# A decoder layer on one core: entry norms in tile order, q strips traced before the next tiles' transposes, v copied by ScalarE, row sums of squares on GpSimd

## The chip, the core and the metric

One core of a Trainium2 chip runs the whole layer. The time is device microseconds of one launch: 1199.61 us is the median of three runs of the kernel before (1198.49 to 1199.99). The core has a matrix engine (TensorE; PE in the profile, PEld for its weight loads), a vector engine (VectorE, DVE), a scalar engine (ScalarE, ACT), GpSimd (POOL), and the queue of SyncE (SP), which issues most of the DMAs. ScalarE issues DMAs too (ACTq in the profile).

## The reference, cut to what matters

All arrays are float32; 1024 tokens, width 1024, 16 heads of 64, of which 8 do stick-breaking attention (sb) and 8 sliding-window attention (swa, with two key/value heads).

```python
h = layer_norm(x, ln_in_g, ln_in_b)
proj = h @ w_in                     # [sb_q | sb_k | sb_v | swa_q | swa_k | swa_v]
sb_out, swa_out = stick_breaking_attention(...), sliding_window_attention(...)
mix = concat([rms_norm(sb_out, g_sb), rms_norm(swa_out, g_swa)]) @ w_out
h = layer_norm(ALPHA * h + mix, ln1_g, ln1_b)
ffn = (silu(h @ w_gate) * (h @ w_up)) @ w_down
out = layer_norm(ALPHA * h + ffn, ln2_g, ln2_b)
```

`rms_norm` divides each token's row of 512 by the root of the mean of its squares; the kernel keeps `sb_out` and `swa_out` transposed (features on partitions), so the sum of squares of a token runs over partitions and strips.

## The kernel before, in words

Each matrix operand is split into a high part (fp32r) and a low part, and a product is three matmuls (`mm3`, L169). Weights come as strips of 128 columns (`strip`, L201, two ahead): SP loads a raw strip into one of two staging buffers, ScalarE casts the high part (L108), GpSimd subtracts the low part (L109).

Entry. SP loads the norm's gain and bias as rows and the first x tiles; TensorE broadcasts the rows over the partitions (L269) and ScalarE copies the four halves out (L270). `entry(t)` (L303) norms the token tile t: VectorE takes the statistics (L141 to L134), GpSimd the power -1/2 (L135). For tiles 0 and 1 VectorE does all the scaling (L151, L154); for the others ScalarE subtracts the mean (L161), VectorE scales (L162) and GpSimd adds the bias (L164). Then TensorE transposes the tile in two groups of four (L117), ScalarE casts the high part (L121), TensorE subtracts it in PSUM (L124) and ScalarE casts the low part (L125). Last, ScalarE's queue stores h (L314). The transposes use two PSUM buffers.

First projections (L554 to L568). For each of four chunks of 256 tokens (two tiles): the swa k strip (`put_k`), the v strip (`put_v`, L339: VectorE copies the product out of PSUM, L343, TensorE transposes it, L346), then `entry` of the next two tiles, the two q strips of the first key/value head, and, from the second chunk on, two blocks of the first attention. Later stages interleave attention (`swa_attend`, `sb_attend`) with the next projections by `merge`, which weighs steps of both. The v of the four pairs of sb heads comes in two chunks of 512 each.

Output projections. `c1_steps` (L598) projects the swa half while the last sb pair's attention runs; then follows the sb half (L646 to L673) with the second norm and the transposes for the feed-forward part. `out_load(g, c)` (L505) loads four strips of one chunk of 256 tokens, casts the high part (ScalarE, L510), subtracts the low part (VectorE, L511) and squares in place (ScalarE, L512). `out_proj` (L515) sums a tile's squares by TensorE against a column of ones, one matmul per strip (L522, in the profile two records each), takes the root (L525, L528), and then does the tile's products (L174), which VectorE scales and adds (L533). Two chunks are loaded ahead.

A planner puts each engine's instructions in order: it runs over a simulated timeline and takes, of those that are ready, the one traced first (attention steps inside `merge` get a head start). The order is then fixed per engine; at run time an engine waits for the next one in its order. `Ordered` (L50) can tie the instructions of one queue to the order in which they are traced; before, it is on for SP in the last stage alone (L813).

Of the kernel before, what the change touches and what calls it, by code (L numbers as in the profile page):

```python
# [49 lines left out]
class Ordered:  # L50
# [12 lines left out]

    def matmul(self, *a, **k):
        self._queue(self.eng.matmul(*a, **k))

    def transpose(self, *a, **k):
        self._queue(self.eng.transpose(*a, **k))

    def dma_start(self, *a, **k):  # L70
        self._queue(self.eng.dma_start(*a, **k))


@with_exitstack
def layer(ctx: ExitStack, tc: tile.TileContext, x, ln_in, w_sw, w_sb, norm_g,
          sinks, rel_bias, onehot, w_out, ln1, w_gu, w_down, ln2, out):
    nc = tc.nc
    pe, act, dve, pool = nc.tensor, nc.scalar, nc.vector, nc.gpsimd
    sp = Ordered(tc, nc.sync)
# [27 lines left out]
    def split_w(raw, hi, lo):  # L107
        act.copy(hi, raw)  # L108
        pool.tensor_tensor(out=lo, in0=raw, in1=_f(hi), op=ALU.subtract)  # L109

    def split_ps(ps, hi, lo):
# [25 lines left out]
    def ln_stats(xt, n=2, eps=LN_EPS):  # L137
        bst = st.tile([P, n, 6], F32, tag=f"bst{n}", name="bst")
        w = D // n
        for i in range(n):  # L140
            dve.bn_stats(out=bst[:, i, :], in_=xt[:, i * w:(i + 1) * w])  # L141
        mv = st.tile([P, 2], F32, tag="mv", name="mv")
        dve.bn_aggr(out=mv, in_=bst)  # L143
        rstd = st.tile([P, 1], F32, tag="rstd", name="rstd")
        rpow(rstd, mv[:, 1:2], 1.0, eps)
        return mv[:, 0:1], rstd

    def ln_apply(dst, xt, g, b, fast=False, eps=LN_EPS):
        mu, rstd = ln_stats(xt, 2, eps)
        if fast:  # L150
            dve.scalar_tensor_tensor(out=dst, in0=xt, scalar=mu, in1=g, op0=ALU.subtract, op1=ALU.mult)  # L151
            for i in range(2):
                h = slice(i * 512, i * 512 + 512)
                dve.scalar_tensor_tensor(out=dst[:, h], in0=dst[:, h], scalar=rstd, in1=b[:, h],  # L154
                                         op0=ALU.mult, op1=ALU.add)
            return
        nmu = st.tile([P, 1], F32, tag="nmu", name="nmu")
        dve.tensor_scalar(out=nmu, in0=mu, scalar1=-1.0, scalar2=None, op0=ALU.mult)
        for i in range(2):
            h = slice(i * 512, i * 512 + 512)  # L160
            act.activation(dst[:, h], xt[:, h], AF.Identity, bias=nmu)  # L161
            dve.scalar_tensor_tensor(out=dst[:, h], in0=dst[:, h], scalar=rstd, in1=g[:, h],  # L162
                                     op0=ALU.mult, op1=ALU.mult)
            pool.tensor_tensor(out=dst[:, h], in0=dst[:, h], in1=b[:, h], op=ALU.add)  # L164

    def bc_load(dst, src):
# [34 lines left out]
    def strip(i, ahead=2):  # L201
        while len(loaded) < min(len(strips), i + ahead):
            i_ = len(loaded)
            raw = w_raw(strips[i_])
            hi, lo = (U([P, KT, P], "whu"), U([P, KT, P], "wlu")) if i_ == 3 else w_tiles()
            split_w(raw, hi, lo)
            loaded.append((hi, lo))
        return loaded[i]
# [57 lines left out]
    for i, dst in enumerate((g_in, b_in)):  # L266
        for h in (slice(0, 512), slice(512, D)):
            ps = bps.tile([P, 512], F32, tag=("pp", "av")[i], name="bc")
            pe.matmul(ps, row1, rows[i][:, h], start=True, stop=True)  # L269
            act.copy(dst[:, h], ps)  # L270
    sink = cst.tile([P, 8], F32, name="sink")
# [30 lines left out]

    def entry(t):  # L303
        xt = xts.pop(t)
        ln_apply(xt, xt, g_in, b_in, t < 2)
        c, o, todo = t // 2, (t % 2) * P, []
# [6 lines left out]
        flush(todo)  # L313
        act.dma_start(h_dram[t], xt)  # L314

# [23 lines left out]
    def put_v(ps, c0, nc_, vts):  # L339

        n = 2 * nc_
        vr = ws.tile([P, n, P], F32, tag="raw", bufs=2, name="vr")
        dve.tensor_copy(vr.rearrange("p a b -> p (a b)"), ps)  # L343
        pv = bps.tile([P, n, 2, 64], F32, tag="pp", name="pv")
# [160 lines left out]
    def out_load(g, c):  # L505
# [6 lines left out]
        act.activation(m, m, AF.Square)  # L512
        return mh, ml, m

    def out_proj(c, m, wo, acc):  # L515
        mh, ml, ss = m
        for i in range(2):
            t = 2 * c + i
            tok = slice(i * P, (i + 1) * P)
            pr = bps.tile([P, 1], F32, tag="pp", name="pr")  # L520
            for k in range(4):
                pe.matmul(pr, ss[:, k, tok], ones, start=(k == 0), stop=(k == 3))  # L522
            var = st.tile([P, 1], F32, tag="var", name="var")
# [29 lines left out]
    att0 = swa_attend(0, q0, kd, kl, vts, bias0)  # L553
    entry(0)  # L554
    entry(1)
    for c in range(4):
# [3 lines left out]
        put_v(ps, c, 1, vts)  # L560
        if c < 3:
            entry(2 * c + 2)
            entry(2 * c + 3)
        swa_q(0, 0, q0, c, 1)
        swa_q(0, 1, q0, c, 1)
        if c > 0:
            next(att0)
# [23 lines left out]
    def load_acc(c, src):  # L591
# [4 lines left out]
        return res  # L596

    def c1_steps():  # L598
        ms = [out_load(1, 0), out_load(1, 1)]
        for c in range(4):  # L600
# [3 lines left out]
            if c < 2:  # L604
                ms.append(out_load(1, c + 2))

    merge(sb_attend(NPAIR - 1, *cur), 72, c1_steps(), 8)
# [38 lines left out]
    order = (0, 2, 1, 3)  # L646
    ms = {c: out_load(0, c) for c in order[:2]}
    hs = {}
# [220 lines left out]
    with tc.tile_pool(name="dn", bufs=4, reuse_waits="tile") as dn:  # L869
# [8 lines left out]
        def one(t):  # L878
            ot = dn.tile([P, D], F32, tag="ot", bufs=2, name="ot")
            rows = slice(t * P, (t + 1) * P)  # L880
            if t < NT - 1:
                ln_apply(ot, h[t], g2, b2)
                nc.sync.dma_start(out[rows, :], ot)
                return
            mu, rstd = ln_stats(h[t], 4)
            for x in (d0, d1):
# [103 lines left out]
```

## Time and profile before

| | us |
|---|---|
| median of three runs | 1199.61 |
| the profiled execution | 1199.59 |
| its span, first to last instruction | 1197.9 |
| TensorE busy | 1154.2 |
| VectorE busy | 837.7 |
| GpSimd busy | 591.8 |
| ScalarE busy | 581.3 |
| mean granted TensorE clock | 0.986 |

The span is cut into stages by what TensorE works on: the entry and first projections until about 100 us, attention with projections until about 380, the output projections until about 560, then the feed-forward part. A busy TensorE is not a TensorE at its peak: matmuls are pipelined, their ends are modelled, and at the lower clock level they take longer.

### The profile page before, as it was taken

The page shows a single profiled execution, that of the slowest core. Times are in us where ns is not written, and L with a number is a line of the kernel's source. Part 1 is how long each engine was busy: PE and PEld are TensorE (multiplying, and loading weights), DVE is VectorE, ACT ScalarE, POOL GpSimd, SP SyncE. Part 2 cuts the span into 40 slices and gives each one's busy share as a digit, 9 for nine tenths or more (in the row PEclk, how much of TensorE's full clock was granted, in tenths as well). Part 3 has the DMA queues.
Part 4 walks back from the last instruction along what each step waited for, and adds up shares of the span by engine and source line. Part 5 has one row for each costly group of instructions (what it writes and reads, how often), then busy time and mean ns, then how long its engine had stood idle before and what let it go on. Part 6 is the DMA issues. An engine that isn't in the chain of part 4 may idle for free. (4 is left out here: it accounts for less than half of the span.)

```text
span 1197.9 us, 17900 instructions
## 1 busy us (share of the span) xinstructions
PE 1154.2 (96%) x6394; PEld 997.9 (83%) x6394; DVE 837.7 (70%) x1291; ACT 581.3 (49%) x1255; POOL 591.8 (49%) x572
## 2 busy tenths in 40 slices
PE   6899999999998998998999999999999999999997
PEld 4888998999998887876888888888888888888885
DVE  8776687887889895866765555564565448899735
ACT  5666577767677654346333232223233224456531
POOL 5623435566646463214777657665577521000584
PEclk9999999999999998999999999999999999999999
DMA  7403012110105525243333223422232339853431
GB/s 249 167 15 93 27 28 76 28 62 25 48 19 182 196 93 191 83 141 141 114 132 114 89 79 115 131 90 96 97 114 97 106 111 388 328 185 106 131 123 70
DMA packets 59913, 140.17 MB, mean 117 GB/s; under 512 B 7046, under 2 KB 18863, under 8 KB 59825
## 3 DMA queue, kind: packets, MB, share of 16 engines
q1 hardware_dynamic: 45264, 110.19, 28.6%
q10 hardware_dynamic: 14560, 28.85, 6.2%
q8 instruction: 50, 0.82, 0.3%
q14 instruction: 39, 0.31, 0.1%
HBM read 95.23 MB, written 41.17 MB: 114 GB/s over the span
## 5 line engine op out<-in xcount | busy, mean ns | idle before, releaser
L109 POOL TENSOR_TENSOR w<-s,w 128x512 fp32r<-128x512 f32 x88 | 124.0, 1412 | 121.4 <-ACT w L108 121.4
L174 PE MATMUL pp<-xh,whi 128*128 128x256 f32 x544 | 157.3, 290 | 1.4 <-DVE q L337 1.4
L174 PE MATMUL pp<-xh,wlo 128*128 128x256 f32 x544 | 157.0, 289 | 0.0
L174 PE MATMUL pp<-xl,whi 128*128 128x256 f32 x544 | 156.6, 288 | 0.0
L108 ACT CAST w<-s 128x512 fp32r<-128x512 f32 x88 | 54.6, 622 | 201.9 <-PE pgu L730 119.9
L803 PE MATMUL pd<-bhl,ahl 128*128 128x512 f32 x612 | 139.2, 389 | 0.0
L803 PEld LDWEIGHTS pd<-bhl,ahl 128*128 128x128 f32 x612 | 114.8, 188 | 24.2 <-DVE bhl L795 0.4
L762 DVE TENSOR_TENSOR t<-t,pgu 128x512 f32<-128x512 f32 x88 | 60.0, 682 | 98.7 <-PE pgu L730 95.6
L454 POOL TENSOR_TENSOR s<-s,s 128x127 f32<-128x127 f32 (+2 forms) x96 | 91.5, 956 | 51.8 <-DVE s L450 25.0
L174 PEld LDWEIGHTS pp<-xh,whi 128*128 128x128 f32 x544 | 105.5, 194 | 2.5 <-DVE q L337 1.7
L174 PEld LDWEIGHTS pp<-xl,whi 128*128 128x128 f32 x544 | 105.2, 193 | 1.5 <-ACT xl L125 0.3
L174 PEld LDWEIGHTS pp<-xh,wlo 128*128 128x128 f32 x544 | 105.2, 193 | 1.3
L795 POOL TENSOR_TENSOR ahl<-ar,ahl 128x512 fp32r<-128x512 f32 x12 | 16.2, 1353 | 134.8 <-ACT ahl L794 134.7
L450 DVE TENSOR_TENSOR_SCAN s<-s,brk 128x128 f32<-128x128 f32 (+1 forms) x64 | 69.4, 1089 | 12.0 <-ACT s L441 11.2
L794 ACT CAST ahl<-ar 128x512 fp32r<-128x512 f32 x63 | 39.1, 622 | 77.1 <-PE pd L803 50.2
L112 ACT CAST at<-tra 128x256 fp32r<-128x256 f32 (+1 forms) x160 | 55.2, 355 | 36.4 <-DVE at L113 19.0
L395 POOL TENSOR_TENSOR L<-L,rd 128x512 f32<-128x512 f32 (+1 forms) x32 | 30.9, 988 | 81.7 <-DVE rd L393 80.0
L109 POOL TENSOR_TENSOR w<-gr,w 128x512 fp32r<-128x512 f32 x44 | 62.2, 1424 | 8.1 <-ACT w L108 8.1
L113 DVE TENSOR_TENSOR at<-tra,at 128x256 fp32r<-128x256 f32 (+1 forms) x160 | 58.8, 382 | 8.8 <-ACT at L112 7.5
L730 PE MATMUL pgu<-B11h,w 128*128 128x512 f32 x176 | 59.1, 397 | 2.1 <-ACT w L108 1.5
L441 ACT ACTIVATE s<-z 128x128 f32<-128x128 f32 (+2 forms) x96 | 47.6, 498 | 23.9 <-PE z L440 15.7
L730 PE MATMUL pgu<-T4h,w 128*128 128x512 f32 x176 | 57.9, 390 | 0.4 <-DVE t L762 0.4
(234 smaller groups left out, 3315.6 us busy)
## 6 DMA issues: line engine op xcount, KB each, us to landing
ar<-a_dram SPq DMA_DIRECT2D x73, 256.0 KB, 3.1
a_dram<-act ACTq DMA_DIRECT2D x33, 512.0 KB, 2.6
gr<-in_w_gu SPq DMA_DIRECT2D x24, 512.0 KB, 3.4
ur<-in_w_gu SPq DMA_DIRECT2D x23, 512.0 KB, 3.5
bq<-in_w_down SPq DMA_DIRECT2D x44, 256.0 KB, 5.2
raw<-in_w_sb SPq DMA_DIRECT2D x12, 512.0 KB, 3.6
h_dram<-x ACTq DMA_DIRECT2D x8, 512.0 KB, 5.2
m<-o_dram SPq DMA_DIRECT2D x32, 128.0 KB, 2.8
```

The lines of the kernel that those rows point to most:

```text
L108: act.copy(hi, raw)
L109: pool.tensor_tensor(out=lo, in0=raw, in1=_f(hi), op=ALU.subtract)
L112: act.copy(hi, ps)
L113: dve.tensor_tensor(out=lo, in0=ps, in1=_f(hi), op=ALU.subtract)
L174: pe.matmul(ps, a, b, start=(i == 0), stop=(i == n - 1))
L441: act.activation(s2[:, 0:w], ps, AF.Sigmoid, scale=-SCALE)
L450: dve.tensor_tensor_scan(s2[:, 0:w][:, ::-1], s2[:, 0:w][:, ::-1], brk[:, 512 - w:][:, ::-1] if last else zero.broadcast_to([P, w]), 1.0 i ...
L454: pool.tensor_tensor(out=s1[:, 0:m], in0=s1[:, 0:m], in1=s2[:, 1:m + 1], op=ALU.mult)
L730: pe.matmul(ps, a, b, start=(start and n == 0), stop=(stop and n == 11), skip_group_check=True)
L762: add = lambda out, x: dve.tensor_tensor(out=out, in0=x, in1=ps, op=ALU.add)
L794: act.copy(w[:, 0], src)
L803: pe.matmul(pd[t], x, y, start=(first and k == 0 and n == 0), stop=(end and k == KF - 1 and n == 2), skip_group_check=True)
```

## The change

The entry is cut into `norm(t)` and `turn_in(t)` (the transposes). `norm(t)`'s statistics are tied behind the last VectorE instruction that tile t-1's norm returns (for tiles 0 and 1 the last scaling, for the others the negated mean). The stores of h for tiles 0 and 1 go to SP, the others stay on ScalarE, and all are issued in `norm`. In each chunk of the first projections the two next tiles are normed before the q strips as before, but transposed after them. The weight strips 0 and 1 are split in halves, and strip 0's casts are tied behind the last copy of the bias. `put_v` copies by ScalarE. `out_load` adds the four strips of squares on GpSimd (two additions), so that `out_proj` needs one matmul against ones. The first chunk of the second output projection is loaded inside `c1_steps`, after its third chunk. `Ordered` passes any operation of its engine through and forgets the last one while it is off; TensorE is wrapped in it, but never turned on.

```diff
-    def matmul(self, *a, **k):
-        self._queue(self.eng.matmul(*a, **k))
...
+    def __getattr__(self, name):
+        f = getattr(self.eng, name)
+        if not self.on:
+            self.last = None
+            return f
+
+        def call(*a, **k):
+            self._queue(f(*a, **k))
+        return call
+
+    def after(self, ins, before):
+        self.tc.add_manual_dep(
+            ins.ins, before.ins.name,
+            mybir.DependencyInfo(mybir.DependencyClass.NoSync, mybir.DependencyReason.DATA),
+            reason="traced order")
...
-    pe, act, dve, pool = nc.tensor, nc.scalar, nc.vector, nc.gpsimd
+    pe, act, dve, pool = Ordered(tc, nc.tensor), nc.scalar, nc.vector, nc.gpsimd
...
     def split_w(raw, hi, lo):
-        act.copy(hi, raw)
+        ins = act.copy(hi, raw)
         pool.tensor_tensor(out=lo, in0=raw, in1=_f(hi), op=ALU.subtract)
+        return ins
...
@@ in strip() @@
-            split_w(raw, hi, lo)
+            for k in (slice(0, 4), slice(4, KT)) if i_ < 2 else (slice(0, KT),):
+                ins = split_w(raw[:, k], hi[:, k], lo[:, k])
+                if i_ == 0:
+                    pe.after(ins, copied)
...
@@ broadcasting g_in, b_in @@
-            act.copy(dst[:, h], ps)
+            copied = act.copy(dst[:, h], ps)
...
-    def entry(t):
+    ended = []
+
+    def norm(t):
+        xt = xts[t]
+        first, last = ln_apply(xt, xt, g_in, b_in, t < 2)
+        if t > 0:
+            for ins in first:
+                pe.after(ins, ended[t - 1])
+        ended.append(last)
+        (act if t > 1 else sp).dma_start(h_dram[t], xt)
+
+    def turn_in(t):
         xt = xts.pop(t)
-        ln_apply(xt, xt, g_in, b_in, t < 2)
         c, o, todo = t // 2, (t % 2) * P, []
...
         flush(todo)
-        act.dma_start(h_dram[t], xt)
...
@@ put_v @@
-        dve.tensor_copy(vr.rearrange("p a b -> p (a b)"), ps)
+        act.copy(vr.rearrange("p a b -> p (a b)"), ps)
...
@@ out_load @@
         act.activation(m, m, AF.Square)
-        return mh, ml, m
+        pool.tensor_tensor(out=m[:, 0:2], in0=m[:, 0:2], in1=m[:, 2:4], op=ALU.add)
+        pool.tensor_tensor(out=m[:, 0], in0=m[:, 0], in1=m[:, 1], op=ALU.add)
+        return mh, ml, m[:, 0]
...
@@ out_proj @@
-            for k in range(4):
-                pe.matmul(pr, ss[:, k, tok], ones, start=(k == 0), stop=(k == 3))
+            pe.matmul(pr, ss[:, tok], ones, start=True, stop=True)
...
-    entry(0)
-    entry(1)
+    norm(0)
+    norm(1)
+    turn_in(0)
+    turn_in(1)
     for c in range(4):
         ps, tok = xmul(strip(0), c, 1)
         put_k(ps, tok, kd, kl)
         ps, tok = xmul(strip(1), c, 1)
         put_v(ps, c, 1, vts)
-        if c < 3:
-            entry(2 * c + 2)
-            entry(2 * c + 3)
+        for t in (2 * c + 2, 2 * c + 3)[:NT - 2 - 2 * c]:
+            norm(t)
         swa_q(0, 0, q0, c, 1)
         swa_q(0, 1, q0, c, 1)
+        for t in (2 * c + 2, 2 * c + 3)[:NT - 2 - 2 * c]:
+            turn_in(t)
...
@@ c1_steps @@
             if c < 2:
                 ms.append(out_load(1, c + 2))
+            elif c == 2:
+                m0.append(out_load(0, 0))
...
-    ms = {c: out_load(0, c) for c in order[:2]}
+    ms = {0: m0[0], order[1]: out_load(0, order[1])}
```

`ln_stats` and `ln_apply` return the instructions that `norm` ties.

## Rows read from the trace of the kernel before

**Rows 1.** The page, part 1: busy time, share of span, instructions of each engine.
```profile
PE 1154.2 (96%) x6394; PEld 997.9 (83%) x6394; DVE 837.7 (70%) x1291; ACT 581.3 (49%) x1255; POOL 591.8 (49%) x572
```

**Rows 2.** By windows, entry: length, then busy of PE, PEld, DVE, ACT, POOL; granted clock, DMA.
```profile
10.00:20.00 10.00, 4.18 (x14) 2.60 (x15) 9.98 (x13) 4.00 (x7) 6.59 (x3) 1.00 0.69 247
20.00:30.00 10.00, 9.27 (x39) 7.53 (x37) 10.00 (x17) 8.12 (x14) 9.20 (x7) 1.00 0.76 284
30.00:40.00 10.00, 8.11 (x58) 6.98 (x59) 7.91 (x20) 7.13 (x17) 8.12 (x7) 1.00 0.76 274
40.00:50.00 10.00, 8.21 (x67) 7.76 (x66) 8.27 (x12) 6.22 (x13) 9.57 (x8) 1.00 0.24 98
...
80.00:100.00 20.00, 15.77 (x104) 13.91 (x103) 12.61 (x29) 15.11 (x45) 9.42 (x9) 0.91 0.13 38
```

**Rows 3.** By windows, around the output projections; columns as in rows 2.
```profile
395.00:430.00 35.00, 34.92 (x209) 30.08 (x208) 29.35 (x53) 20.75 (x55) 21.10 (x34) 1.00 0.54 182
...
465.00:476.00 11.00, 7.46 (x25) 5.74 (x24) 4.37 (x8) 5.56 (x9) 1.91 (x2) 0.69 0.63 225
476.00:500.00 24.00, 24.00 (x143) 21.03 (x142) 19.39 (x37) 8.08 (x16) 4.79 (x6) 1.00 0.26 94
```

**Rows 4.** Timeline of the entry: start, us, engine, line, operation; in brackets idle time before.
```profile
7.57 1.91 PE L269 MATMUL bc<-row,row 1*128 1x512 f32 x2
...
8.93 1.27 DVE L151 SCALAR_TENSOR_TENSOR x<-x,mv,g_in 128x1024 f32<-128x1024 f32 x1
...
10.34 0.75 DVE L154 SCALAR_TENSOR_TENSOR x<-x,rstd,b_in 128x512 f32<-128x512 f32 x1
10.54 2.76 POOL L109 TENSOR_TENSOR wlo<-raw,whi 128x1024 fp32r<-128x1024 f32 x1 [2.10 <-ACT whi L108]
...
11.07 3.32 DVE L151 SCALAR_TENSOR_TENSOR x<-x,mv,g_in 128x1024 f32<-128x1024 f32 x1
...
11.59 0.58 ACT L270 COPY b_in<-bc 128x512 f32<-128x512 f32 x1
...
14.30 1.27 DVE L141 BATCH_NORM_STATS2 bst<-x 128x6 f32<-128x512 f32 x2
...
15.50 2.17 DVE L154 SCALAR_TENSOR_TENSOR x<-x,rstd,b_in 128x512 f32<-128x512 f32 x1
...
17.71 1.35 DVE L154 SCALAR_TENSOR_TENSOR x<-x,rstd,b_in 128x512 f32<-128x512 f32 x2
```

**Rows 5.** Timeline, around 35 us, a store of h on ScalarE's queue.
```profile
34.40 0.33 ACTq L314 DMA_DIRECT2D h_dram<-x  x1
...
35.40 0.50 PE L124 MATMUL trx<-xh,negi 128*128 128x512 f32 x1 [0.94 <-ACT xh L121]
```

**Rows 6.** Timeline, around 467 us, between the two output projections.
```profile
465.76 1.04 ACT L510 CAST whi<-m 128x1024 fp32r<-128x1024 f32 x1 [6.22 <-DMA m<-o_dram]
...
467.13 0.39 PE L487 MATMUL av<-at,v 128*128 128x256 f32 x1 [1.50 <-ACT at L112]
...
470.18 1.87 PE L522 MATMUL pr<-ones,m 128*128 128x1 f32 x8 [1.11 <-ACT m L512]
```

**Rows 7.** Timeline, around 399 us: one tile's row sums.
```profile
399.02 0.95 PE L522 MATMUL pr<-ones,m 128*128 128x1 f32 x8
```

**Rows 8.** Groups by form: xcount, busy us, mean ns, then idle time before them.
```profile
L742 POOL TENSOR_TENSOR act<-act 128x512 f32<-128x512 f32 x11 | 17.6, 1598 | 0.7
L454 POOL TENSOR_TENSOR s<-s,s 128x511 f32<-128x511 f32 x16 | 17.5, 1091 | 1.2
...
L522 PE MATMUL pr<-ones,m 128*128 128x1 f32 x128 | 16.4, 245 | 3.8 <-DVE res L533 2.7 <-ACT m L512 1.1
...
L454 POOL TENSOR_TENSOR s<-s,s 128x255 f32<-128x255 f32 x16 | 10.7, 669 | 0.8
...
L343 DVE COPY vr<-pp 128x512 f32<-128x512 f32 x8 | 5.4, 678 | 0.2
```

**Rows 9.** Waits: who waited for whom, total us, times, longest us.
```profile
PEld pv L346 <- DVE vr L343: 5.9, 5, 2.2
```

More of the change, by code (lines that the diff above doesn't have):

```diff
@@ L62, in _queue @@
         self.last = ins.ins
-    def matmul(self, *a, **k):
-        self._queue(self.eng.matmul(*a, **k))
[L67 to L71, printed above, removed]
+    def __getattr__(self, name):
[11 more added lines that the diff above has]
+            reason="traced order")
 @with_exitstack
@@ L138, in ln_stats @@
         bst = st.tile([P, n, 6], F32, tag=f"bst{n}", name="bst")
-        w = D // n
+        w, first = D // n, []
         for i in range(n):
-            dve.bn_stats(out=bst[:, i, :], in_=xt[:, i * w:(i + 1) * w])
+            first.append(dve.bn_stats(out=bst[:, i, :], in_=xt[:, i * w:(i + 1) * w]))
         mv = st.tile([P, 2], F32, tag="mv", name="mv")
@@ L145, in ln_stats @@
         rpow(rstd, mv[:, 1:2], 1.0, eps)
-        return mv[:, 0:1], rstd
+        return mv[:, 0:1], rstd, first
     def ln_apply(dst, xt, g, b, fast=False, eps=LN_EPS):
-        mu, rstd = ln_stats(xt, 2, eps)
+        mu, rstd, first = ln_stats(xt, 2, eps)
         if fast:
@@ L153, in ln_apply @@
                 h = slice(i * 512, i * 512 + 512)
-                dve.scalar_tensor_tensor(out=dst[:, h], in0=dst[:, h], scalar=rstd, in1=b[:, h],
-                                         op0=ALU.mult, op1=ALU.add)
-            return
+                last = dve.scalar_tensor_tensor(out=dst[:, h], in0=dst[:, h], scalar=rstd, in1=b[:, h],
+                                                op0=ALU.mult, op1=ALU.add)
+            return first, last
         nmu = st.tile([P, 1], F32, tag="nmu", name="nmu")
-        dve.tensor_scalar(out=nmu, in0=mu, scalar1=-1.0, scalar2=None, op0=ALU.mult)
+        last = dve.tensor_scalar(out=nmu, in0=mu, scalar1=-1.0, scalar2=None, op0=ALU.mult)
         for i in range(2):
@@ L164, in ln_apply @@
             pool.tensor_tensor(out=dst[:, h], in0=dst[:, h], in1=b[:, h], op=ALU.add)
+        return first, last
     def bc_load(dst, src):
@@ L596, in load_acc @@
         return res
+    m0 = []
     def c1_steps():
@@ L884, in one @@
                 return
-            mu, rstd = ln_stats(h[t], 4)
+            mu, rstd, _ = ln_stats(h[t], 4)
             for x in (d0, d1):
```

## The prediction

> **What bounds the kernel now.** I read the page first. TensorE is busy 1154.2 of 1197.9 us [rows 1]: at most 44 us is idle, and whatever shortens the kernel either fills that idle time or takes work off TensorE. The view by windows says where the idle time lies. TensorE is busy 4.18 of 10 us in 10 to 20, then 9.27, 8.11 and 8.21 of 10 up to 50, and 15.77 of 20 in 80 to 100 [rows 2]: the entry (norms, transposes, first projections) holds about 14 us of it. In 395 to 430 and in 476 to 500 TensorE is full to within 0.1 us; between them, in 465 to 476, it stands for 3.5 us and the granted clock is 0.69 [rows 3]. With levels of 1.2 and 2.4 GHz, 0.69 means 62% of the 11 us, 6.8 us, at the lower level, so up to 3.4 us more was lost after the idle time. The timeline of the entry [rows 4, 5] and that of the boundary at 465 [rows 6] show which engine was late.
>
> **The change part by part, on the profiled execution's 1199.59 us** (span 1197.9, 1.7 around it; the median shown is 1199.61, so the sum may be read against either).
>
> *Sums of squares.* Each of 16 tiles now issues 8 matmul records for `pr` (4 strips, two records each), 0.95 us in a burst [rows 7], so 0.95/8 = 0.12 us apiece; the group has 128 records [rows 8]. The change leaves 2 per tile: 6 x 0.119 = 0.71 us less, 11.4 us over 16 tiles. They lie in stretches where TensorE is full, so this is on the path; 11.4 is the ceiling. Added: per out_load (8 of them) two GpSimd additions, 128x512 and 128x256. The nearest rows are 1.09 and 0.67 us (the product of two s tiles), the dearest like one 1.60 [rows 8]: 1.8 to about 2.6 us each time, 14 to 21 us of GpSimd in all. GpSimd works 21.10 of 35 us in the first full stretch and 4.79 of 24 in the second [rows 3], so it has room. The added wait: `pr` comes 2 us or more after ScalarE's square, and what queues behind `pr` on TensorE is the tile's whole projection. Two chunks are loaded ahead, some ten microseconds of matmuls, which covers it; only the first chunk has no such cover. There I charge up to 2 us. A second cost is VectorE: the row of a 1024-wide scalar_tensor_tensor is 1.27 us alone and 3.32 us when it started inside a GpSimd split of 2.76 us; it ended 1.1 us after the split did [rows 4]. So a GpSimd addition can hold back a VectorE instruction for its length. VectorE is at 29.35 of 35 us [rows 3], so some of this returns as late PSUM drains. Bounds: -11.4 (all of it kept) to +3 (nothing saved, the first wait and delays paid). I take -8.5, three quarters, because TensorE is the full engine in both stretches.
>
> The Trainium skill, "SBUF — State Buffer", section "Who interferes with whom", says that a VectorE instruction with two SBUF inputs and a GpSimd instruction that reads SBUF exclude each other for the whole instruction, by issue order. By that rule the trace agrees (3.32 against 1.27), and it speaks against this part; the second rival below is what it would make of it.
>
> *Entry.* Today the last b_in copy comes at 11.59, after two weight casts, although the broadcast matmuls end at 7.57 + 1.91 = 9.48. The new edge puts that copy first: 9.5 + 0.58 = 10.1. The second half of x0 then takes 0.75 and is ready at 10.9, not at 15.50 + 2.17 = 17.67 [rows 4]. x1's statistics now wait for that: 10.9 + 1.27 + about 0.4 for the small instructions = 12.5, and then 1.27 + 2 x 0.75 = 2.8 us of scaling: 15.3 if GpSimd leaves VectorE alone. Beside it GpSimd splits strips 0 and 1, now in four halves of about 1.3 us (half of the 2.76); each of the three VectorE instructions can wait for one: +3.9, 19.2. Today x1 ends at 17.71 + 1.35 = 19.06. So x1 comes between 3.8 us earlier and not at all earlier; the middle is 1.9. x0 has by then been transposed and cast, and TensorE needs only x1's eight transposes. I take 2 us for the earlier start.
> Then the order "two q strips, next tiles' norms underneath, their transposes after": today the transposes of x2 and x3 stand in front of the q matmuls and TensorE waits there, for instance 0.94 us for a cast on ScalarE that had itself been queued behind the store of h, issued at 34.40 [rows 5]. 20 to 50 has 0.73 + 1.89 + 1.79 = 4.4 us idle [rows 2]. With q first, some 5.8 us of matmuls (48 at about 0.12) cover the norms. But the transposes then meet the next k strip with nothing between, and each group of four needs two ScalarE casts of 0.58. The stores for tiles 2 to 7 stay on ScalarE's queue and are now traced before the tile's turn: the same wait, no better. I take half of the 4.4, so -2, and nothing for 80 to 100.
> Hidden: halved casts cost ScalarE a fixed part twice (under 0.5 us in all), before TensorE needs strip 0. The stores of x0 and x1 go to SP: x0's is ready near 11, before SP's next strip load, which today waits for GpSimd to 13.3 (the split's end in [rows 4]); x1's can hold the last x loads for a few us, which are needed far later. If that cover is gone, a late strip 2 or 3 costs its delay, 2 to 4 us. Bounds of the entry: -3.8 - 4.4 = -8.2 to +5 (no earlier start, three turns each waiting for casts 1.6 us longer). I take -4.
>
> *v copied by ScalarE.* 12 copies leave VectorE (8 at 0.68 [rows 8], 4 smaller ones) for ScalarE, where a 128x512 copy out of PSUM takes 0.58 [rows 4]. The weight loads of v's transposes waited for VectorE 5.9 us in 5 places [rows 9]. ScalarE is in order too and carries the casts of the same stretch, so I expect most of this wait to change owner. Bounds: -5.9 to +6 (half a microsecond on each of 12). I take -1.
>
> *First chunk of the second projection loaded early.* At 465.76 ScalarE ended a wait of 6.22 us for m's load; behind it stood the `at` casts, and TensorE idled 1.50 us for one and 1.11 us for the square before `pr` [rows 6]. The edit moves one of two such loads: four SP loads, two ScalarE instructions, one VectorE subtraction, now the two additions, forward into the third quarter of the first projection, where SP's queue holds stores and weight loads that are not yet due. The second chunk's load keeps its place, and its cast can block ScalarE the same way; then only the 1.11 goes. Bounds: -6.9 (3.5 idle and 3.4 of clock) to +1. I take -1.5.
>
> The other edits (returned instructions, one order edge less at the start of SP's ordered stretch) I cost at nothing; the one freed load runs under a full TensorE.
>
> **Sum:** -8.5 - 4 - 1 - 1.5 = -15.0: 1199.6 - 15.0 = 1184.6 us.
>
> **Rivals.**
> 1. *The entry gives nothing.* The order of each engine is planned by readiness, so tracing q first may leave the order as it is, or the transposes meet the k strip bare; GpSimd's splits hold x1 to 19. For it: VectorE and GpSimd already take turns there [rows 4]. Against: x0 is surely earlier. Time: 1199.6 - 8.5 - 1 - 1.5 + 1 for a worse turn = 1189.6.
> 2. *VectorE becomes the bound beside the additions.* In the first stretch VectorE stands at 84%; four loads of 1.8 us of additions in about 85 us hold it for up to 8% more, and shorter TensorE work (5.7 us of 85) makes that 84/0.93 + 9 = 99%. Then the first half of the 11.4 is not kept, and -3.5 remains for the sums: 1199.6 - 3.5 - 4 - 1 - 1.5 = 1189.6. Against: many VectorE instructions there read PSUM, and the row does not show those held. The Trainium skill's rule above ("SBUF — State Buffer", "Who interferes with whom") is this rival's ground.
> 3. *Slower: v's copies become late on ScalarE.* Place: the 8 wide copies in the projections of the stick-breaking part. If each stands behind a cast or an exponential and costs TensorE 1.9 us (5.9/5 = 1.2 is today's mean, 2.2 the longest [rows 9]) and is followed by 3.4 us at the lower clock level (half of the 6.8 from [rows 3]), 1.7 lost, that is 8 x 3.6 = 29 us, less the 5.9 and about 4 of clock paid today: +19. With the other terms 1199.6 + 19 - 14 = 1204.6. It decides from about 3 us per copy. Against: ScalarE is the less busy engine of the two over the whole [rows 1].
>
> **Chances.** Forecast 0.60 (its own range 1179 to 1190), rival 1 0.20, rival 2 0.13, rival 3 0.07. The range 1177 to 1196 takes in the first three with their spread and leaves out the third and the tails. A change under 0.2% (2.4 us) cannot be told from none. Forecast and rivals 1 and 2 are faster but for about 0.05 of their tails within 0.2%; rival 3 is 0.06 slower, 0.01 same: faster 0.88, same 0.06, slower 0.06.
>
> **What would show it.** Sums: 32 `pr` records in place of 128, bursts of about 0.25 us, and the stretch from the first `pr` to the last projection matmul shorter by 8 to 9 us with TensorE still full. Entry: x0's last scaling ends near 11, x1's before 18, the dense k matmuls start 2 us earlier; idle time in 20 to 50 near 2. v: no VectorE copy, the waits of v's transposes now on ScalarE, of much the same sum. Boundary: the 6.22 us wait gone or halved. The prediction is wrong if the projection stretch does not shrink (rival 2), or if new idle time stands in front of v's transposes (rival 3), or if a TensorE wait for casts opens at each turn of the entry loop (rival 1).

## The result, and the profile after

The changed kernel takes 1192.94 us (median of 8 runs, 1191.97 to 1198.09); beside it on the same chip the kernel before took 1200.31 (8 runs, 1198.49 to 1202.41). The ratio over all of these runs is 0.9947, 95% interval 0.9933 to 0.9961: 6.4 us faster (the two medians are 7.4 apart), where 15.0 were forecast. The profiled execution went from 1199.59 to 1192.77 us, its span from 1197.9 to 1191.1.

First the page after, its busy line, beside [rows 1]:

```profile
PE 1143.3 (96%) x6298; PEld 983.7 (83%) x6298; DVE 830.7 (70%) x1279; ACT 585.6 (49%) x1269; POOL 614.8 (52%) x590
```

TensorE has 96 records fewer, those of the sums, and is busy for 10.9 us less. Not all of that is the sums': the changed kernel without the sums edit (below) is busy for 1150.6 us, 7.3 more, and two other pairs that differ in the sums alone give 8.8 and 8.5, against the forecast's ceiling of 11.4. The span shrank by 6.8, so TensorE now stands for 4.1 us longer than before. The same windows as in [rows 2, 3] show where:

```profile
10.00:20.00 10.00, 5.54 (x17) 2.75 (x16) 5.59 (x10) 5.82 (x11) 6.45 (x5) 1.00 0.86 315
20.00:30.00 10.00, 8.19 (x56) 7.19 (x55) 9.17 (x20) 7.08 (x12) 9.10 (x7) 1.00 0.91 326
30.00:40.00 10.00, 4.20 (x21) 3.26 (x20) 9.87 (x22) 6.30 (x14) 9.15 (x9) 0.79 0.39 146
40.00:50.00 10.00, 7.96 (x53) 7.36 (x53) 7.44 (x8) 3.94 (x10) 8.81 (x6) 0.87 0.33 133
80.00:100.00 20.00, 18.85 (x145) 17.43 (x145) 11.89 (x29) 17.12 (x50) 8.46 (x7) 1.00 0.08 18
395.00:430.00 35.00, 34.19 (x188) 28.53 (x188) 27.87 (x53) 20.15 (x49) 22.75 (x33) 1.00 0.52 177
465.00:476.00 11.00, 8.64 (x38) 6.96 (x38) 5.80 (x13) 4.62 (x8) 4.25 (x5) 0.85 0.75 244
476.00:500.00 24.00, 22.15 (x119) 18.57 (x118) 21.34 (x39) 5.98 (x13) 7.96 (x7) 1.00 0.23 88
```

In 10 to 20 TensorE has 1.4 us more work than before: the earlier start is there. In 30 to 40 it lost that and more: 4.20 busy us where 8.11 stood, and the clock fell to 0.79 behind it. 80 to 100 gained 3.1. The stretch 476 to 500, which was full, has 1.85 us of idle time (the changed kernel is further on by then: its first matmul of the second output projection, `woh`, comes at 462.9, before at 471.9).

Three waits stand out; the first is in the entry (timeline after, the rows of four engines):

```profile
30.59 5.97 POOL L172 TENSOR_TENSOR x<-x,b_in 128x512 f32<-128x512 f32 x4
30.92 3.29 DVE L170 SCALAR_TENSOR_TENSOR x<-x,rstd,g_in 128x512 f32<-128x512 f32 x2
34.37 0.72 ACT L169 ACTIVATE x<-x,nmu 128x512 f32<-128x512 f32 x1 [3.53 <-DVE nmu L166]
35.61 0.35 ACT L364 COPY vr<-pp 128x256 f32<-128x256 f32 x1
36.02 0.69 PE L367 MATMUL pv<-ident,vr 128*128 128x128 f32 x2 [5.11 <-ACT vr L364]
```

Read upwards: TensorE waits 5.11 us for the first chunk's v; the copy stands on ScalarE behind the mean subtraction of x5; that one waits for VectorE's `nmu`, and the two scalings of x4 ahead of it took 1.65 us each beside GpSimd's b_in additions (one of the same form took 0.73 at 27.27 with GpSimd at its short `rstd`). The tiles are counted by their statistics (x2 at 19.32, x3 at 21.01, x4 at 26.07, x5 at 28.28): x4 and x5 are traced behind the q strips, yet their norms were planned ahead of v's copy. The Trainium skill, "SBUF — State Buffer", section "Who interferes with whom", has the two engines exclude each other for such instructions; 1.65 against 0.73 agrees.

The second wait opens the first output projection, where ScalarE's square of the first chunk ended at 374.0:

```profile
376.39 0.85 POOL L475 TENSOR_TENSOR s<-s,s 128x383 f32<-128x383 f32 x1
377.21 1.26 POOL L534 TENSOR_TENSOR m<-m 128x512 f32<-128x512 f32 x1
378.41 0.18 POOL L478 COPY carry<-s 128x1 f32<-128x1 f32 x1
378.55 0.72 POOL L535 TENSOR_TENSOR m<-m 128x256 f32<-128x256 f32 x1
379.33 0.58 PE L544 MATMUL pr<-ones,m 128*128 128x1 f32 x2 [2.56 <-POOL m L535]
```

The third is in the second projection, where a GpSimd addition lies beside VectorE's norm (L162 takes 2.81 us for two; 0.75 is one alone):

```profile
480.40 1.28 POOL L534 TENSOR_TENSOR m<-m 128x512 f32<-128x512 f32 x1
480.54 2.81 DVE L162 SCALAR_TENSOR_TENSOR res<-res,rstd,b 128x512 f32<-128x512 f32 x2
481.75 1.05 POOL L535 TENSOR_TENSOR m<-m 128x256 f32<-128x256 f32 x1
484.07 0.39 PE L509 MATMUL av<-at,v 128*128 128x256 f32 x1 [1.85 <-DVE at L121]
```

At the boundary that [rows 6] showed, ScalarE still waits 5.51 us for the second chunk's load (6.22 before); TensorE's idle time in 465 to 476 went from 3.5 to 2.4 us:

```profile
469.46 1.04 ACT L531 CAST whi<-m 128x1024 fp32r<-128x1024 f32 x1 [5.51 <-DMA m<-o_dram]
470.83 0.39 PE L508 MATMUL av<-at,v 128*128 128x256 f32 x1 [1.10 <-ACT at L120]
```

### The profile page after: what moved, and what is told of

Its sections match the earlier page's. It is cut to its first block, busy times and chain, and to the rows that moved or that the text cites. A ratio compares the mean times of both kernels' runs of the same rounds, so it can differ in the third digit from the quotient of the medians.

```text
span 1191.1 us, 17726 instructions
## 1 busy us (share of the span) xinstructions
PE 1143.3 (96%) x6298; PEld 983.7 (83%) x6298; DVE 830.7 (70%) x1279; ACT 585.6 (49%) x1269; POOL 614.8 (52%) x590
## 5 line engine op out<-in xcount | busy, mean ns | idle before, releaser
L759 PE MATMUL pgu<-T2h,w 128*128 128x512 f32 x176 | 58.0, 390 | 0.7 <-ACT w L115 0.7
```

Source lines behind the costliest of these rows:

```text
L759: pe.matmul(ps, a, b, start=(start and n == 0), stop=(stop and n == 11), skip_group_check=True)
```

## The experiments

Line numbers with the old entry are those of the kernel before, or a few more. All ratios are to the kernel before on the same chip; 0.0010 is 1.2 us, and intervals are about 0.001 to 0.0016 to either side, so a difference between two ratios is uncertain by some 2 us. The order on each engine is planned anew for each kernel: an edit in the entry moves the order of all that follows, one in the projections leaves the order of the entry and the strips as it was. The times there still differ from one execution to the next: in the changed kernel and five others of the same order up to there, the last matmul of the strips starts at 372.4 to 375.1 us.

**Each edit alone, and each taken out of the changed kernel.** v's copies alone (the first diff below):

> The kernel before with v's copies on ScalarE and nothing else. Theory A (in the wide copies ScalarE is the freer engine, which gave the changed kernel some 6 us in the attention stage; the narrow ones in the entry stand behind norms only in the changed order): 3 to 7 us faster than the kernel before, 1193 to 1197 us. Forecast of the prediction: 1 us faster. Rival B (the narrow copies cost in the old order as well): within 2 us of the kernel before, with a new wait for ScalarE in front of v's transposes in the entry.

0.9981 (0.9972 to 0.9991): 2.3 us, less than theory A's 3 to 7 and just above rival B's 2, whose new wait in the entry is there, but short (0.76 us at 35.81). In its trace the first `wo` matmul (first output projection) comes at 377.8 against 386.6, 8.8 us earlier; the first `woh` matmul at 470.6 against 471.9, 1.3 earlier. Of a gain of 8.8 most had gone by the boundary. Timeline there:

```profile
457.61 3.66 SPq L71 DMA_DIRECT2D m<-o_dram  x8
462.29 1.05 ACT L510 CAST whi<-m 128x1024 fp32r<-128x1024 f32 x1 [3.71 <-DMA m<-o_dram]
466.18 1.04 ACT L510 CAST whi<-m 128x1024 fp32r<-128x1024 f32 x1 [2.07 <-DMA m<-o_dram]
468.50 0.80 PE L522 MATMUL pr<-ones,m 128*128 128x1 f32 x3 [2.90 <-ACT m L512]
```

The loads left SP at 457.6, hardly earlier than the 458.9 of the kernel before. So the early chunk was tried alone, the entry edit alone (all of the change's diff but the lines of `put_v`, `m0` and the sums), and v with the early chunk (both diffs here):

```
-        dve.tensor_copy(vr.rearrange("p a b -> p (a b)"), ps)
+        act.copy(vr.rearrange("p a b -> p (a b)"), ps)
```
```
+            elif c == 2:
+                m0.append(out_load(0, 0))
...
-    ms = {c: out_load(0, c) for c in order[:2]}
+    ms = {0: m0[0], order[1]: out_load(0, order[1])}
```

> The kernel before with the first chunk of the second out-projection loaded early and nothing else. Theory A (the changed kernel crossed this boundary, from the seventh to the eighth 24th of the projections, in 9.0 us against 13.0 before, and nothing is given back behind it): 3 to 5 us faster than the kernel before. Forecast of the prediction: 1.5 us faster. Rival B (the second chunk's load holds ScalarE as long as the first's did, and the changed kernel's gain there came from the sums): within 1 us of the kernel before.

> The kernel before with the changed entry alone: norms in tile order on VectorE, q strips first, then the next tiles' transposes; v's copies stay on VectorE, the sums on TensorE, no early chunk. Theory A (the entry edit gives nothing by itself: with v's narrow copies back on VectorE the changed kernel reached the 14th group of 24 matmuls at 96.7 us, which the kernel before with v on ScalarE reached at 96.6 without the entry edit): within 2 us of the kernel before, at the end of the first four strips no more than 1 us ahead of it. Rival B (the forecast: 4 us faster, spoiled in the changed kernel by v's copies alone): 3 to 5 us faster.

> The kernel before with two of the four edits: v's copies on ScalarE and the first chunk loaded early. Theory A (v on ScalarE gained 7.5 us up to the end of the strips and 8.8 at the first projection matmul, and gave all of it back at the boundary near 470, where ScalarE stands 3.7 and 2.1 us for m's loads and TensorE 2.9 for pr; the early load takes this wait away): 6 to 10 us faster than the kernel before, 1190 to 1194 us. Rival B (something else, SP's queue or the last pair's stores, sets when the boundary is crossed, whatever comes earlier): 2 to 4 us faster, as with v's copies alone.

The early chunk: 0.9979 (0.9968 to 0.9990), 2.5 us, below theory A's 3 to 5: in its trace 3.5 us ahead near 488, of which 1.4 are left at the end. The entry: 0.9983 (0.9973 to 0.9993), 2.0 us, within theory A's 2 at the end; but its other sign (no more than 1 us ahead at the end of the first four strips) failed. It is 3.6 us ahead there (the 384th projection matmul at 103.5, before at 107.1) and 3.4 at the first `wo` matmul, of which 0.7 are left at the first `woh` matmul. v and early chunk together: 0.9941 (0.9927 to 0.9955), 7.1 us, within theory A and more than 2.3 + 2.5. The wait for m's load had swallowed what v's copies gained; without the early chunk the first `woh` matmul came at 470.0 to 471.9 in five kernels (before, and with v, the entry, the sums, or all three of them), with it at 459.1 to 465.8 in all that had been ahead at the first `wo` matmul.

The sums alone (the diff here on the kernel before), and the changed kernel without each edit in turn (its diff taken back):

```
+        pool.tensor_tensor(out=m[:, 0:2], in0=m[:, 0:2], in1=m[:, 2:4], op=ALU.add)
+        pool.tensor_tensor(out=m[:, 0], in0=m[:, 0], in1=m[:, 1], op=ALU.add)
-        return mh, ml, m
+        return mh, ml, m[:, 0]
...
-            for k in range(4):
-                pe.matmul(pr, ss[:, k, tok], ones, start=(k == 0), stop=(k == 3))
+            pe.matmul(pr, ss[:, tok], ones, start=True, stop=True)
```

> The kernel before with the sums edit alone. Theory A (the boundary near 470 waits for m's load whatever comes before, and the first chunk's additions cost 2.8 us): 1 to 4 us faster than the kernel before. Forecast of the prediction: 8.5 us faster. Rival B (GpSimd's additions hold VectorE so much that nothing is kept): within 1 us of before.

> The changed kernel with the sums of squares back on TensorE, four matmuls for each tile, no GpSimd additions. Theory A (most of the 10.9 us that TensorE no longer works was given back at the first chunk's added wait, its low clock and VectorE waiting for GpSimd): 1 to 5 us slower than the changed kernel, 1194 to 1198 us. Rival B (the sums kept three quarters, as predicted, and the missing gain is elsewhere): 8 to 11 us slower, 1201 to 1204 us.

> The changed kernel with all of v's copies back on VectorE. Theory A (v on ScalarE is worth 2 to 5 us, as alone and beside the early chunk): 2 to 5 us slower than the changed kernel, 0.997 to 0.999 of before. Rival B (in the new entry it costs what it gains in the strips): within 1.5 us of the changed kernel.

> The changed kernel without the early load of the second out-projection's first chunk. Theory A (the wait for m's load at the boundary near 470 is worth most when all before it is faster): 4 to 8 us slower than the changed kernel, 0.998 to 1.001 of before. Rival B (as alone): 2 us slower.

> The changed kernel without the entry edit, all else as in it (v on ScalarE, early chunk, all sums by GpSimd). Theory A (the entry edit costs 2 to 5 us in this company): 1188 to 1191 us, 0.990 to 0.993 of the time before. Rival B (the entry edit is neutral and the kernel with six loads summed was faster for the first two loads alone): 0.994 to 0.996, within 1.5 us of the changed kernel.

| edit | forecast, us | alone | changed kernel without it | so its worth there, us |
|---|---|---|---|---|
| sums on GpSimd | -8.5 | 0.9980 (-2.4) | 0.9954 | -0.8 |
| entry | -4 | 0.9983 (-2.0) | 0.9941 | +0.7 |
| v on ScalarE | -1 | 0.9981 (-2.3) | 0.9972 | -3.0 |
| early chunk | -1.5 | 0.9979 (-2.5) | 0.9983 | -4.3 |

Theory A holds for the sums alone and, in the changed kernel, for v and for the early chunk; for the sums there the 0.8 lies just below its 1 to 5. For the entry rival B holds, neutral in the changed kernel. The two terms forecast small were worth most in company, and the two forecast large next to nothing there.

**Where the sums' gain went.** First the additions of the first two loads were taken back, then all additions left out, then all moved to VectorE:

```
 act.activation(m, m, AF.Square)
+if g == 1 and c < 2: return mh, ml, m     # four matmuls per tile for these
 pool.tensor_tensor(out=m[:, 0:2], ...)    # left out / dve. in the other two
```

> The changed kernel, but the first two chunks of the first output projection are summed by TensorE (four matmuls for each tile, no additions for these two loads). Theory A (the first chunk's additions, 377.2 to 379.3, are the added wait): the idle time of 2.56 us at 379.33 goes, part of the 3.4 us of clock behind it too, and 4 tiles x 0.7 us of matmuls come back: 2 to 4 us faster than the changed kernel, 1189 to 1191 us. Rival B (GpSimd's scan work holds the start of this stage by itself: another wait takes the place): 0 to 3 us slower, for the matmuls that come back.

> The changed kernel without the two GpSimd additions of each load; the sum of squares is then that of the first strip alone (left out: the other three strips). TensorE does the two records for each tile as in the changed kernel. Theory A (TensorE is the full engine there and the additions ate the gain, through the first chunk's wait and through VectorE): 5 to 9 us faster than the changed kernel, 1184 to 1188 us. Rival B (the stage is not bound by TensorE alone, another engine's chain sets its length): no more than 3 us faster, which is the first wait.

> The changed kernel with the two additions of each load on VectorE in place of GpSimd. Theory A (the additions cost 4 us because they stand in GpSimd's queue behind the scan's work, 377.2 for a square that ended at 374.0, and hold VectorE): 2 to 5 us faster than the changed kernel, near the one without additions (1187.1 us of span), first group of projection matmuls back at 379 to 380 us. Rival B (VectorE, 84% busy there, has no room for 8 x 1.6 us): within 2 us of the changed kernel or slower, with new waits for VectorE in the first out-projection.

First two loads by TensorE: 0.9926 (0.9911 to 0.9941), 2.5 us better than the changed kernel, and the wait of 2.56 is gone. Without any addition: 0.9910 (0.9896 to 0.9925), 4.4 better, between theory A's 5 to 9 and rival B's 3: that is their price here, against a saving on TensorE that is worth 5.3 (0.9954 to 0.9910). The traces place it. The changed kernel, the one without additions and the one without the sums edit all start the last matmul of their strips at 372.4 to 372.5. The first `wo` matmul follows at 382.12, 379.32 and 379.31, the last `woh` matmul at 537.04, 532.78 and 536.99. So 2.8 of the additions' 4.3 us are there at the first `wo` matmul and 1.5 come behind it; and from the first `wo` to the last `woh` matmul the four matmuls for each tile cost 4.2 us, not 11.4. On VectorE: 0.9926 (0.9911 to 0.9940). The total is as theory A had it, but its reason falls: with the additions on VectorE `pr` waited 2.48 us all the same.

```profile
380.76 0.35 PE L544 MATMUL pr<-ones,m 128*128 128x1 f32 x2 [2.48 <-DVE m L535]
```

It is the added step behind the square that is late at the first chunk, not GpSimd's queue alone.

Then the same sums without the new entry, beside v and the early chunk, for six of the eight loads (`if g == 1 and c < 2` as above) and for two (`if g == 0 or c < 2`):

> The kernel before with v's copies on ScalarE, the first chunk loaded early, and GpSimd's additions for all loads but the first two (these are summed by TensorE); the entry is the old one. Theory A (the sums are kept in the first out-projection, where the changed kernel without additions gained 5.1 of 5.7 us, at 0.7 us for each of 4 tiles; in the second they give nothing): 2 to 4 us faster than v and early chunk together (0.9941 of before), 0.991 to 0.993 of the time before. Rival B (the additions cost as much as they save once the first wait is gone): 0.994 or more. Rival C (the whole 8.5 for 12 tiles in 16): 0.988.

> As the kernel with v on ScalarE, the early chunk and the additions for all loads but the first two, but GpSimd adds for two loads alone, the third and fourth of the first out-projection; the whole second out-projection is summed by TensorE. Theory A (in the second out-projection TensorE's saved time turns into waits and the additions hold VectorE): as fast as with six loads added or up to 3 us faster. Rival B (TensorE's saved 0.7 us for each of 8 tiles is kept there): 4 to 6 us slower than with six loads.

Six loads: 0.9890 (0.9874 to 0.9906), 1187.41 us, 13.2 us faster than before: the fastest kernel here, 0.57% ahead of the changed one, and more than theory A's 2 to 4 beside v and early chunk (rival C's 0.988 is nearest). It added 6.1 us to v and early chunk (0.9941), and 0.71 x 12 = 8.5 is the ceiling for its 12 tiles: the forecast's three quarters would be 6.4. In the new entry's company the same six loads are worth 3.4 (0.9954 to 0.9926). Two loads: 0.9942, no better than none and 6.2 us behind six: rival B's figure, theory A of that run is wrong. All eight loads (the kernel without the entry edit above): 0.9941. The first two loads' additions thus cost there as much as the other six give; in the trace the wait is the same 2.56 us, and the span is 4.7 us longer. 1.6 of it are there at the first `wo` matmul, though the strips had ended 0.8 us earlier. The rest comes late, where the two differ in the clock. Windows of the kernel with six loads, then with eight:

```profile
455.00:500.00 45.00, 41.64 (x219) 34.56 (x218) 37.42 (x68) 16.59 (x34) 17.26 (x17) 1.00 0.38 135
500.00:535.00 35.00, 32.93 (x177) 25.65 (x175) 27.01 (x46) 19.61 (x41) 9.37 (x9) 1.00 0.39 136
535.00:620.00 85.00, 80.46 (x355) 64.66 (x356) 56.62 (x58) 36.81 (x70) 61.11 (x43) 1.00 0.38 130
```

```profile
455.00:500.00 45.00, 41.15 (x209) 33.74 (x209) 37.53 (x67) 16.72 (x34) 19.00 (x21) 0.96 0.39 135
500.00:535.00 35.00, 33.43 (x166) 26.83 (x165) 25.90 (x44) 16.36 (x33) 9.26 (x9) 0.95 0.37 135
535.00:620.00 85.00, 81.00 (x363) 65.07 (x362) 59.37 (x65) 38.33 (x74) 58.68 (x40) 0.98 0.39 130
```

(1 - 0.96) x 45 + (1 - 0.95) x 35 + (1 - 0.98) x 85 = 5.3 us are lost to the lower level in the second and none in the first, with about as much idle time in both. Over the whole of the two executions the clock is the same, 0.992: the kernel with six loads is at 0.94 in 0 to 60 and at 0.96 in 372 to 455, the other at 1.00 and 0.98, which by the same sum is 6.9 us against 1.7, part of it beside waits. The kernels with two loads and with none lose about 5.2 us each by the same sum (their clocks are 1.00, 0.90, 0.98 and 0.96, 0.95, 0.98), so the 6.1 us of the six loads may rest in part on a clock that holds in this stage; how much reaches the end is not shown.

**Why the entry gave nothing.** v's narrow copies were put back on VectorE, and in another kernel the norms of tiles 2 and 3 were taken off ScalarE and GpSimd:

```
-        act.copy(vr..., ps)
+        (dve.tensor_copy if nc_ == 1 else act.copy)(vr..., ps)
```
```
-        first, last = ln_apply(xt, xt, g_in, b_in, t < 2)
+        first, last = ln_apply(xt, xt, g_in, b_in, t < 4)
```

> The changed kernel, but v's four narrow copies in the entry go back to VectorE; the eight wide ones stay on ScalarE. Theory A (the entry lost what it had gained because v's copy stood on ScalarE behind the next tile's mean subtraction, which stood behind VectorE and GpSimd taking turns): the idle time of 5.11 us at 36.02 goes and the 3.4 us lost at the lower clock behind it go too, less 0.5 us for each of four copies waiting on VectorE: 4 to 8 us faster than the changed kernel, 1185 to 1189 us by the profiled 1192.8. Rival B (the entry is held by the norms themselves; only the owner of the wait changes): VectorE works the same queue of norm instructions, so v's copy waits there as long: within 1.5 us of the changed kernel.

> The changed kernel, but the norms of tiles 2 and 3 take the form of tiles 0 and 1: the whole scaling on VectorE (four instructions of 0.75 us for a tile), no subtraction on ScalarE and no b_in addition on GpSimd for them. Theory A (v's copy stands idle because VectorE's scaling of x3 and x4 takes 1.65 us an instruction beside GpSimd's b_in additions instead of 0.73, and holds ScalarE): v's transposes in the entry wait 2 us or less in place of 5.1 (3.0 with the copy on VectorE), and the group of matmuls behind them comes 2 to 4 us earlier; the end, planned anew, 1 to 4 us earlier. Rival B (it is the number of norm instructions ahead of the strip's copies, on whichever engine): the scaling now costs VectorE as much as the turn-taking did, the wait stays between 3 and 5 us.

VectorE's copy: 0.9989 (0.9980 to 0.9998), slower than the changed kernel. The owner of the wait changed, not the wait:

```profile
36.57 0.69 PE L367 MATMUL pv<-ident,vr 128*128 128x128 f32 x2 [3.87 <-DVE vr L364]
```

Rival B was right on the place, and my reason (ScalarE's queue) does not explain the wait; for the time neither held: TensorE did 3.7 us more in 22 to 60, but the strips behind, planned anew, took 217.1 us from 164 on where the changed kernel took 207.9. In all nine kernels with this entry, v by either engine, these transposes came at 35.9 to 37.0 us, after waits of 1.5 to 5.1: on the whole, the earlier TensorE arrived, the longer it waited. Six of the nine have the same order up to there, and the wait still went from 1.5 to 5.1 in them: the 5.11 is the longest, and one trace is no measure of its length. Norms on VectorE: the transposes came at 31.70 with no wait at all, and TensorE did 6.1 us more in 22 to 60. Windows of the changed kernel, then of this one:

```profile
22.00:60.00 38.00, 28.40 (x201) 26.47 (x202) 28.91 (x54) 21.62 (x47) 25.34 (x20) 0.91 0.47 176
60.00:110.00 50.00, 47.89 (x376) 45.44 (x375) 33.33 (x82) 37.84 (x113) 15.15 (x13) 1.00 0.16 49
```

```profile
22.00:60.00 38.00, 34.51 (x230) 32.23 (x229) 30.62 (x58) 22.63 (x55) 20.30 (x16) 0.91 0.48 176
60.00:110.00 50.00, 45.59 (x359) 43.16 (x358) 35.95 (x81) 36.19 (x105) 18.51 (x15) 1.00 0.17 53
```

That fits the turn-taking of VectorE and GpSimd as what held v's copy, but does not show it by itself, because the plan changed too: ScalarE now has v's copy ahead of the mean subtractions of x4 and x5.

```profile
31.09 0.38 ACT L364 COPY vr<-pp 128x256 f32<-128x256 f32 x1 [0.87 <-PE pp L183]
35.42 1.34 ACT L169 ACTIVATE x<-x,nmu 128x512 f32<-128x512 f32 x2
```

The end did not move: 0.9940 (0.9925 to 0.9954); 2.3 us went in 60 to 110, and two waits for PSUM drains in the second projection (2.23 and 3.53 us) took more.

The kept traces show something else on the entry. The start of the first wide v transposes, near 180 us, in every kernel but the two with `t < 4`, by entry and by the engine of v's narrow copies:

| | narrow copies on VectorE | on ScalarE |
|---|---|---|
| old entry | 183.1 to 184.2 (3 kernels) | 179.4 to 181.6 (5) |
| new entry | 181.2 to 182.0 (3) | 182.5 to 185.1 (6) |

Each of the two edits brings this point forward by itself, both together do not; within a group the order up to there differs little or not at all, so its spread shows how far executions differ. The new entry and v's copies on ScalarE stand in each other's way in the entry; by which queue is not shown.

The same norms (`t < 4`) in the fastest kernel, whose entry is the old one:

> The old entry with v on ScalarE, the early chunk and GpSimd's additions for all loads but the first two (0.989 of before), and the norms of tiles 2 and 3 wholly on VectorE. Theory A (the norms' turn-taking of VectorE and GpSimd holds the entry, old or new): v's first transposes at 30 to 33 us in place of 35.4, the matmuls at 60 us 2 to 4 us further on, the end 0.986 to 0.988 of before. Rival B (what is gained there is given back in the strips and the projections, whose order is planned anew): the transposes earlier as in A, the end at 0.989 to 0.993. Rival C (in the old entry TensorE itself, not the norms, comes to v's transposes at 35 to 36): no change in the entry.

1.0016 (1.0007 to 1.0025), and the transposes at 37.70: all three theories missed.

```profile
28.26 3.50 DVE L154 SCALAR_TENSOR_TENSOR x<-x,rstd,b_in 128x512 f32<-128x512 f32 x2 [0.32 <-POOL rstd L135]
31.79 0.33 ACTq L314 DMA_DIRECT2D h_dram<-x  x1
32.16 0.58 ACT L125 CAST xl<-trx 128x512 fp32r<-128x512 f32 x1 [2.85 <-DVE x L154]
32.79 0.39 PE L174 MATMUL pp<-xl,whi 128*128 128x256 f32 x1 [3.74 <-ACT xl L125]
```

x3's store of h stands on ScalarE's queue until x3's norm ends, a cast of `trx` stands behind the store, and TensorE behind the cast, as in [rows 5] but four times as long. VectorE's scalings took 1.75 us each here too, beside GpSimd's weight split (2.50 us from 28.71). At the matmuls of 42 us this kernel is 4 us behind the fastest one; how the other 10 came about behind that was not followed.

## Why the prediction was wrong

The sign was right; the sum was more than twice what came, because its two largest terms failed.

**Sums, -8.5.** Two steps failed. The first is "three quarters, because TensorE is the full engine in both stretches": with nothing added, TensorE's shorter work was worth 5.3 us, under half of the 11.4. Between these two traces TensorE is busy for 7.0 us less (1150.6 to 1143.6) and the span is 4.2 shorter; the rest became idle time. The second is the cover, the charge of "up to 2 us" for the first chunk: the additions cost 4.4, which leaves 0.8. Taking back those of the first two loads gave 2.5 us (new entry) and 6.1 (old entry), each net of the 4 x 0.71 = 2.8 us of matmuls that come back; the wait of 2.56 is part of what they cost. The stretch from the first `pr` to the last projection matmul, forecast 8 to 9 us shorter, went from 162.1 to 157.7. Rival 2's mechanism, VectorE held by the additions, is seen at 480.5 (2.81 us for two in place of 1.5); by these traces it can have no more than the 1.5 us of the additions' price that come behind the first `wo` matmul. With the first two loads left on TensorE, and the old entry, 6.1 were measured for three quarters' 6.4. That this is so near is in part luck, as the 3.4 with the new entry shows; how much of it is the saved work and how much the clock was not separated.

**Entry, -4.** x0 came as worked out: its last scaling ended at 10.96 (forecast 10.9), where [rows 4] had 17.67. x1 did not:

```profile
10.88 1.28 DVE L149 BATCH_NORM_STATS2 bst<-x 128x6 f32<-128x512 f32 x2
11.50 5.92 POOL L116 TENSOR_TENSOR wlo<-raw,whi 128x512 fp32r<-128x512 f32 x4 [1.65 <-ACT whi L115]
17.39 0.57 POOL L143 TENSOR_TENSOR rstd<-mv,mhalf 128x1 f32<-128x1 f32 x1
17.99 1.42 DVE L162 SCALAR_TENSOR_TENSOR x<-x,rstd,b_in 128x512 f32<-128x512 f32 x2 [4.14 <-POOL rstd L143]
```

Its statistics began at 10.88, but its `rstd` stood on GpSimd behind the weight splits, a step that the sum left out: x1 ended at 19.41, later than before (19.06), where rival 1 had it (19). The first k matmul came 0.7 us earlier, not 2. And that "some 5.8 us of matmuls" cover the norms failed: not the new transposes were late, as rival 1 had it, but v's, behind the norms of x4 and x5. What start was won was spent waiting there. The step that the sum got wrong beyond these is to add the entry and v's copies as if they were independent: without v's copies on ScalarE the new entry was 3.6 us ahead at the end of the first four strips, near the forecast's 4, and lost most of that at the boundary; with them it had gained nothing by the wide v transposes. Rival 1's figure for the entry (1 us slower) is about what was measured in this company (+0.7; -2.0 alone). The forecast with rivals 1 and 2 both would have been 1199.6 - 3.5 - 1 - 1.5 + 1 = 1194.6; I held them to be alternatives. That this is near the measured time is in part luck: the sums gave less than its 3.5, v and the early chunk more than its 1 and 1.5.

**v on ScalarE, -1.** Mis-sized: -2.3 alone, -3.0 and more in company. That most of this wait would "change owner" failed: of the waits in [rows 9], those at 195, 319 and 381 us (1.93, 0.58, 1.74 by the trace) went, and 0.44 at 375 is what came in the wide copies. Rival 3 did not happen there. The wait of 5.11 in the entry is a new one; in the kernel before TensorE came to these transposes without any:

```profile
35.74 0.38 PE L346 MATMUL pv<-ident,vr 128*128 128x128 f32 x2
```

So the forecast's sign "on ScalarE, of much the same sum" came true by luck. The after view of waits, with the entry's as nearly all of it:

```profile
PEld pv L367 <- ACT vr L364: 6.7, 4, 5.3
```

**Early chunk, -1.5.** Wrong in kind more than in size: costed as one wait of its own, it decides whether anything gained earlier reaches the end. "The second chunk's load keeps its place" was right: 5.51 of the 6.22 us of ScalarE's wait remain, so the sign "gone or halved" failed. It mattered little: TensorE had the first chunk's matmuls to run meanwhile.

Open: why the same waits brought the clock down in one trace and not in another (below), why the entry and v's copies do not add, where TensorE's saved time went in the projections, and how much of each late loss is the new order rather than the edit.

## What to carry to other kernels

When a stage ends in a wait for something issued at a fixed place (here m's load, traced behind the whole first output projection), gains ahead of it do not add up until that wait is moved: price it first, and try edits in its company, not alone. Work moved to an idle engine adds its latency at each place where nothing is loaded ahead; leave it where it was for the first pieces. And when an order is planned as a whole, compare kernels that differ only late, or the place of an early edit, before believing a small difference at the end.

## What the runs showed of the hardware

The granted clock does not follow the waits alone. The two kernels with six added loads, with the new entry and with the old, have the same waits in the second projection (1.27, 1.80 and 1.26 us; 1.27, 1.85 and 1.26), yet the windows of the first show 0.96, 0.95 and 0.98, those of the second 1.00 throughout (above):

```profile
455.00:500.00 45.00, 41.28 (x210) 34.03 (x209) 34.84 (x64) 15.87 (x33) 17.72 (x20) 0.96 0.41 144
500.00:535.00 35.00, 33.38 (x163) 26.60 (x163) 25.97 (x44) 15.23 (x32) 10.25 (x10) 0.95 0.35 124
535.00:620.00 85.00, 81.48 (x366) 65.46 (x366) 61.63 (x65) 39.67 (x76) 59.66 (x40) 0.98 0.40 135
```

That is 5.3 us by the same sum as above, more than any one of the four edits was worth, and it makes 4.3 us of difference between those two kernels (0.9926 and 0.9890) a poor measure of the entry edit. The clock also differs between executions of one kernel: the six of the first had a mean granted clock of 0.989 to 0.997, and took 1194.00 us at 0.989 and 1188.24 at 0.997; the four of the second had 0.992 to 0.994. A window of one trace is one execution's clock.
